# First norm and projections of a two-layer trunk: both token halves together, in six banks

## The chip, the cores and the metric

The kernel runs on one core of a Trainium2 chip. The metric is the time of one execution on the device, in microseconds (us). Five engines work side by side, each through its own list of instructions in a fixed order: PE (TensorE, matrix products and transposes), DVE (VectorE), ACT (ScalarE), POOL (GpSimd) and SP (SyncE, which here issues the DMAs). They wait for each other by semaphores. SBUF holds the operands, PSUM the sums of PE, in eight banks; in this kernel a bank holds 128 rows of 512 fp32 numbers.

## The reference

The input x has 1024 tokens (S) of 1024 features (D). There are two layers; the first mixes tokens by attention with a forget gate (16 heads of 64), the second by gated linear attention, and each ends with a feed-forward layer. Every sub-layer begins with an RMS norm, whose result is scaled and shifted by columns that come from a conditioning vector c. All is fp32. Only the start of the first layer matters here:

```python
c_act = jax.nn.silu(c)
mod = c_act @ ada_w[i] + ada_b[i]                  # 1024 x 6144 weights
sh1, sc1, g1, sh2, sc2, g2 = jnp.split(mod, 6, axis=-1)
h = modulate(rms_norm(x, norm1_g[i]), sh1, sc1)    # norm * (1 + sc1) + sh1
proj = h @ w_in
q, k, v, f_logit = jnp.split(proj, [D, 2 * D, 3 * D], axis=-1)
log_f = jax.nn.log_sigmoid(f_logit + b_f)
cum = jnp.cumsum(log_f, axis=1)                    # over the tokens
logits = q @ k^T * scale + cum[query] - cum[key]   # per head, causal, softmax, times v
```

So the first scores need all of x normed, sh1 and sc1 of every feature, the f logits of all tokens (the running sum `cum`), and q and k of the first heads.

## The kernel before

Features are cut into eight tiles of 128 (index d), tokens into eight tiles of 128 (`xt[0]` to `xt[7]`), which form two halves of 512 (`hf` 0 and 1). Products of fp32 numbers are made of three matmuls: every operand is split into a high part and a low part, and `mm3` (L236–239) adds high × high, high × low and low × high into one bank.

The part before attention works as follows.

- `load_x` (L274) loads a token tile, 512 KB; `load_ada0` (L280) loads the columns of `ada_w` for sh1 and sc1 of one feature tile d in four DMAs of 256 KB. All go out on SP's queue, in the order in which they stand there.
- `ss_half(hf)` (L436) makes the norm of one half: ACT squares and sums four token tiles (L439), DVE and POOL make the reciprocal root (L441, L442), and the four tiles are scaled in place. In the first half DVE, ACT and POOL share that work; in the second POOL scales all four (L450).
- `ada0_mod(d)` (L455) makes sh1 and sc1 of feature tile d. That is a product of a 1024 × 256 piece of `ada_w` with the vector c. For the first `NPE[d]` of its eight row blocks PE does it directly (L462); the rest is summed on DVE by one instruction for each block (L468, L470), and PE adds the rows of the sum (L472). DVE then writes `modc` (L473) and `amul` (L333), the shift and the scale columns.
- `h_block(d, hf)` (L476) transposes four blocks of 128 × 128 of one half on PE (L479) into a bank of the ring `tp0`, ACT applies scale and shift (L481: `y`) and rounds it to the high part `h0h` (L483), and DVE (even d) or POOL (odd d) subtracts to get the low part `h0l` (L484).
- `first_k(d, hf, acc)` (L489) adds feature tile d into the f, q and k banks of one half: two matmuls for f (L491, L492) and three each for q and k (L237 to L239), 128 × 512 each. q and k are those of the first two heads.
- `first_v` (L811) adds feature tile d into the v banks of the first half, 12 matmuls of 128 × 256 (L817 to L819).
- `first_evac` (L776) empties the f, q and k banks. For the second half it also makes `log_f`, its running sum (a scan along the tokens), writes that to DRAM and loads it back, spread over the partitions (`load_cum`, L802).
- `v_half(g, half)` (L855) computes v of a half for group g of heads, by token tiles; its banks come from the ring `pj` of the attention stage, which are the last two of the eight.
- `load_w` (L190) loads a weight tile and splits it: ACT rounds, POOL subtracts three quarters and DVE one quarter (L205). `feed.next()` calls it for the next weight tiles in line.

In this order: first the norm of the first half, then the loop over d (L829 to L852), in which each pass makes the columns and `h_block` of d + 1, `first_k(d, 0)` and `first_v(d − 1)`; at d = 4 (`XD`) the second half's token tiles are loaded and normed. Behind the loop the first half is evacuated, and a second loop runs `h_block` and `first_k` of the second half. Then come v of the second half (`v_half(0, 1)`), and attention, in which the q and k of the next heads are woven between the scores. `ada0.q` holds the steps for the other columns of the first layer's modulation (`ada_steps`, L336; on DVE L367, L369), which fill in from there.

The program is written in this order, and a scheduler then fixes the order of each engine's list, moving an instruction ahead of others where it reckons that engine free. So the lists hold, for instance, matmuls of v between those of the second half.

PSUM before attention: the ring `par` has five banks (f, q, k and the two v accumulators of the first half, then f, q, k of the second half), `tp0` two banks for transposes, `mp0` one for the columns.

Of the kernel before, what the change touches and what calls it, by code (L numbers as in the profile page):

```python
# [9 lines left out]
F32 = mybir.dt.float32  # L10
# [6 lines left out]
P = 128  # L17
# [36 lines left out]
def trunk(ctx, tc, x, c, ada_w, ada_b, norm1_g, norm2_g, ffn_w_in, ffn_w_out,  # L54
          fox_w_in, fox_b_f, fox_w_out, gla_w_in, gla_w_a2, gla_b_a, gla_g_o,
          gla_w_out, final_g, out, dbg=None, stop=None):
    nc = tc.nc
# [209 lines left out]
    adr = Ring(big, adr_sl + mrows[1:] + acc_sl + s1_sl)  # L267
    mrows = Views(mrows[:1], 8, [P], "mrows").v
    wst = Ring(big, take(6))
    par, tp0, mp0 = ps_rings(5, 2, 1)  # L270

    xt = [xr([P, D], F32, f"xt{t}") for t in range(8)]

    def load_x(t):  # L274
        nc.sync.dma_start(xt[t], x[0, psl(t), :])
# [4 lines left out]
    def load_ada0(d):  # L280
        for kh in range(2):
            t = adr([P, 4, 2, P], F32, f"adas{d}{kh}")
            for j in range(2):
                nc.sync.dma_start(t[:, :, j, :], adaw[0, :, 4 * kh:4 * kh + 4, j, d, :])
            araw[(d, kh)] = t
# [20 lines left out]
    wq0 = load_w(W[:, 0:P], "wq0", wst)  # L306
    wk0 = load_w(W[:, D:D + P], "wk0", wst)
    load_ada0(1)
    load_ada0(2)

    vps = mp0([P, 160], F32, "vps")
    nc.tensor.transpose(vps[:, P:P + 32], rows2, ident[0:32, 0:32])
# [23 lines left out]
    def ada_steps(l, j, acc_of, raw_of, w):  # L336

        steps = deque((c0, k) for c0 in range(0, D, w) for k in range(8))
        got = deque()

        def load():
            if steps:
                c0, k = steps.popleft()
                raw = raw_of([P, w], F32, f"ada{l}{j}{c0}{k}")
                nc.sync.dma_start(raw, ada_w[l, psl(k), j * D + c0:j * D + c0 + w])
                got.append(raw)

        for c0 in range(0, D, w):
            acc = acc_of([P, w], F32, f"acc{l}{j}{c0}")
            for k in range(8):  # L350
                if w == D or c0 == k == 0:
                    load()
                raw = got.popleft()
                if w < D:
                    load()
                    yield ADA_A
                    if k == 0:
                        nc.scalar.mul(acc, raw, cact[:, 0:1])
                    else:
                        nc.scalar.mul(raw, raw, cact[:, k:k + 1])  # L360
                        nc.gpsimd.tensor_add(acc, acc, raw)  # L361
                    yield ADA_B
                    continue
                for q in range(0, w, 256):
                    cs = slice(q, q + 256)
                    if k == 0:
                        nc.vector.tensor_scalar(acc[:, cs], raw[:, cs], cact[:, 0:1], None, op0=ALU.mult)  # L367
                    else:
                        nc.vector.scalar_tensor_tensor(acc[:, cs], raw[:, cs], cact[:, k:k + 1], acc[:, cs],  # L369
                                                       op0=ALU.mult, op1=ALU.add)  # L370
                yield 1.0
            if w < D:
                yield ADA_B
            n, b = w // P, c0 // P
            mp = pj([P, n], F32, f"mp{l}{j}{c0}")
            for k in range(n):
                nc.tensor.matmul(mp[:, k:k + 1], acc[:, psl(k)], ones, start=True, stop=True)
            o = l * 48 + j * 8 + b
            nc.vector.tensor_add(modc[:, l, j, b:b + n], mp, vec[:, o:o + n])
# [54 lines left out]
    hT = new_h("h0")  # L434
# [14 lines left out]
            else:  # L449
                nc.gpsimd.tensor_scalar(xt[t], xt[t], r, 1.0, op0=ALU.mult, op1=ALU.mult)  # L450

    VLAG, XD = 1, 4
    NPE = (4, 4, 4, 0, 0, 0, 0, 0)

    def ada0_mod(d):  # L455

# [19 lines left out]
    def h_block(d, hf):  # L476
        tp = tp0([P, HALF], F32, f"xp{d}{hf}")
        for i in range(4):
            nc.tensor.transpose(tp[:, psl(i)], xt[4 * hf + i][:, psl(d)], ident)  # L479
        y = yv()  # L480
        nc.scalar.activation(y, tp, AF.Identity, scale=acol(0, 0, d), bias=mcol(0, 0, d))  # L481
        hi, lo = hT[d].hi[:, hsl(hf)], hT[d].lo[:, hsl(hf)]
        nc.scalar.copy(hi, y)  # L483
        (nc.gpsimd if d % 2 == 1 else nc.vector).tensor_sub(lo, y, hi.bitcast(F32))  # L484

    def first_acc(hf):
        return [(w, par([P, HALF], F32, f"{nm}s{hf}")) for nm, w in (("f", wf), ("q", wq0), ("k", wk0))]

    def first_k(d, hf, acc):  # L489
        ps = acc[0][1]  # L490
        nc.tensor.matmul(ps, wf[:, d, :], hT[d].hi[:, hsl(hf)], start=d == 0, stop=False)  # L491
        nc.tensor.matmul(ps, wf[:, d, :], hT[d].lo[:, hsl(hf)], start=False, stop=d == 7)  # L492
        for w, ps in acc[1:]:
            mm3(ps, w.hi[:, d, :], w.lo[:, d, :], hT[d].hi[:, hsl(hf)], hT[d].lo[:, hsl(hf)], d == 0, d == 7)
# [271 lines left out]
    feed = Weights(loads)  # L766
# [6 lines left out]
    vts = {}  # L773
    wvs = {}

    def first_evac(hf, acc):  # L776
        cs = hsl(hf)
        f = zt[:, cs]
        sum16(f, ze[:, cs], acc[0][1])
        nc.scalar.activation(ze[:, cs], f, AF.Abs, bias=bf)  # L780
        nc.vector.tensor_scalar(zt[:, cs], f, bf, 0.0, op0=ALU.add, op1=ALU.min)
        nc.scalar.activation(ze[:, cs], ze[:, cs], AF.Exp, scale=-1.0)
        if hf:
            nc.scalar.activation(ze, ze, AF.Ln, bias=1.0)
            nc.vector.tensor_sub(zt, zt, ze)
            nc.vector.tensor_tensor_scan(cum, zt, zt, 0.0, ALU.add, ALU.bypass)
            nc.sync.dma_start(cum_d, cum)
            load_cum(0)
            load_cum(1)
        q_evac(acc[1][1], qkt[0], hf)  # L790
        k_evac(acc[2][1], qkt[0], hf)

    def v_split(g, tp, ps):
        v = vring([P, 2, 4, 2, 64], FR, f"v{g}{tp}")
        src = ps.rearrange("p t (h d) -> p t h d", h=4)
        for i in range(2):
            split(v[:, i, :, 0, :], v[:, i, :, 1, :], src[:, i])
        vts[g].append(v)
# [4 lines left out]
        cums[h] = cumr([P, S], F32, f"cum{h}")  # L803
        nc.sync.dma_start(cums[h], cum_d[h].partition_broadcast(P))

    vts[0] = []
    ss_half(0)
    acc = first_acc(0)
    vacc = [par([P, 2, 256], F32, f"vps0{tp}") for tp in range(2)]

    def first_v(d):  # L811
        wv = wvs[0][d // 4]
        for tp in range(2):
            for i in range(2):
                ts_ = psl(2 * tp + i)
                p_, a_ = vacc[tp][:, i, :], (hT[d].hi[:, ts_], hT[d].lo[:, ts_])
                nc.tensor.matmul(p_, a_[0], wv.hi[:, d % 4, :], start=d == 0 and i == 0, stop=False)  # L817
                nc.tensor.matmul(p_, a_[0], wv.lo[:, d % 4, :], start=False, stop=False)
                nc.tensor.matmul(p_, a_[1], wv.hi[:, d % 4, :], start=False, stop=d == 7 and i == 1)  # L819

    def pre(d):
        ada0_mod(d)
        if d + 3 < 8:
            load_ada0(d + 3)
        h_block(d, 0)

    pre(0)
    for d in range(8):
        if d == 0:  # L829
            feed.depth = 1  # L830
            wvs[0] = [feed.next()]
        if d == 2:
            wvs[0].append(feed.next())
        if d < 7:
            pre(d + 1)
        first_k(d, 0, acc)
        if d >= VLAG:
            first_v(d - VLAG)
        if d == XD:
            for t in range(4, 8):  # L840
                load_x(t)
            ss_half(1)
    for d in range(8 - VLAG, 8):
        first_v(d)
    first_evac(0, acc)
    acc = first_acc(1)
    for tp in range(2):
        v_split(0, tp, vacc[tp])
    h_block(0, 1)
    for d in range(8):  # L850
        if d < 7:
            h_block(d + 1, 1)  # L852
        first_k(d, 1, acc)
    first_evac(1, acc)
    def v_half(g, half):  # L855

        if g not in vts:
            vts[g] = []
        if g not in wvs:
            wvs[g] = [feed.next(), feed.next()]  # L860
        for tp in range(2 * half, 2 * half + 2):
            ps = pj([P, 2, 256], F32, f"vps{g}{tp}")
            for i in range(2):
                yield from proj_tok(ps[:, i, :], wvs[g], hT, 2 * tp + i)
            v_split(g, tp, ps)
        if g or half:
            del wvs[g]
# [122 lines left out]

    for j in (2, 3, 4, 5):
        ada0.q.append(ada_steps(0, j, acc_r, wr, D))
    run(v_half(0, 1))
    for p in range(7):
        parts = [qk_proj(p + 1, 0), qk_proj(p + 1, 1)]
# [757 lines left out]
    wv = [feed.next(), feed.next()]  # L1753
# [18 lines left out]
    for h in range(4):  # L1772
# [102 lines left out]
```

## Time and profile before

| What | us |
|---|---|
| median of three runs | 2450.28 (2445.8 to 2456.89) |
| profiled execution | 2455.79 |
| its span | 2454.1 |
| PE busy | 2393.3 |
| DVE busy | 1697.8 |
| ACT busy | 1193.6 |
| POOL busy | 1153.2 |

The span is the time from the first to the last record of the profile; the profiled execution's own time is a little longer than the span. Busy times are sums over the instructions of an engine. In the rows, a name such as `L472` is a line of the code before, `out<-in` names the tiles, `x4` is a number of records (an fp32 matmul leaves two), and what stands in brackets is the idle time ahead of an instruction and what ended it. The profile's `issue` stands for time in which an engine waited for nothing that the records show. The granted clock is TensorE's, as a share of full speed, averaged over the stretch.

### The profile page before, as it was taken

What the parts mean: (1) busy time and instruction counts of PE and PEld (TensorE: products, weight loads), DVE (VectorE), ACT (ScalarE), POOL (GpSimd) and SP (SyncE); (2) the same over time, 40 slices, a digit from 0 to 9 for tenths busy, and PEclk for the clock granted to TensorE, in tenths of its full rate; (3) what the DMA queues carried; (4) which work ended last, traced back from release to release, by engine and by line L of the source; (5) the groups of instructions that cost most, each with busy time, mean ns of one, the idle gap of its engine ahead of it and who ended that gap; (6) DMA issues with size and microseconds to landing.
All of it is one profiled execution on the core that took longest, in us unless ns stands there. A gap on an engine that the chain in (4) does not pass through costs nothing.

```text
span 2454.1 us, 35528 instructions
## 1 busy us (share of the span) xinstructions
PE 2393.3 (98%) x12458; PEld 2038.0 (83%) x12458; DVE 1697.8 (69%) x2849; ACT 1193.6 (49%) x2281; POOL 1153.2 (47%) x1006
## 2 busy tenths in 40 slices
PE   6999999999999999999999999999999999999998
PEld 6788888888887878888888888888888888888888
DVE  6477777776687777665787555446587767665787
ACT  4565665675454443345324765564344333435325
POOL 4233333332348776653263634442326666653362
PEclk9999999999999999999999999999999999999999
DMA  8223333233426554347665333335325444347664
GB/s 268 79 87 121 96 98 117 70 95 112 131 99 204 180 170 162 129 173 256 233 202 169 100 95 95 95 104 172 102 72 195 143 137 153 125 160 265 229 213 148
DMA packets 318203, 359.19 MB, mean 146 GB/s; under 512 B 18044, under 2 KB 246552, under 8 KB 318024
## 3 DMA queue, kind: packets, MB, share of 16 engines
q1 hardware_dynamic: 318024, 356.92, 43.7%
q8 instruction: 98, 1.61, 0.3%
q14 instruction: 81, 0.66, 0.1%
HBM read 268.19 MB, written 88.67 MB: 145 GB/s over the span
## 4 chain that ended last, share of the span: by engine, by line
PE 79%; DVE 8%; DMA 4%; ACT 3%; POOL 3%; issue 2%; SPq 0%; DVEq 0%; POOLq 0%; ACTq 0%
PE p_b L237 14%; PE p_b L239 14%; PE p_b L238 14%; PE o_b L947 2%; PE t_b L933 2%; PE qk_b L237 2%; PE qk_b L238 2%; PE qk_b L239 2%; DMA ad_s<-in_ada_w_dram 2%; POOL ad_s L361 1%; PE s_b L902 1%; PE s_b L903 1%; PE vps_b L237 1%; PE vps_b L239 1%; PE vps_b L238 1%
## 5 line engine op out<-in xcount | busy, mean ns | idle before, releaser
L160 DVE TENSOR_TENSOR o_s<-xv_s,o_s 128x512 fp32r<-128x512 f32 (+1 forms) x376 | 326.4, 872 | 87.5 <-ACT o_s L159 87.0
L159 ACT CAST o_s<-xv_s 128x512 fp32r<-128x512 f32 (+1 forms) x376 | 217.4, 587 | 304.4 <-PE p_b L239 261.2
L237 PE MATMUL p_b<-B,o_s 128*128 128x512 f32 x608 | 237.2, 393 | 6.3 <-DVE x L1285 3.8
L238 PE MATMUL p_b<-B,o_s 128*128 128x512 f32 x608 | 238.3, 392 | 0.0
L239 PE MATMUL p_b<-B,o_s 128*128 128x512 f32 x608 | 238.0, 392 | 0.0
L913 POOL TENSOR_SCALAR lp_s<-lp_s,st 128x128 f32<-128x128 f32 (+7 forms) x128 | 96.0, 756 | 295.2 <-DVE st L912 274.9
L683 POOL TENSOR_TENSOR ex_s<-xv_s,xv_s 128x512 f32<-128x512 f32 (+1 forms) x64 | 90.6, 1415 | 255.1 <-DMA xv_s<-in_ffn_w_in_dram 93.2
L237 PE MATMUL p_b<-T,o_s 128*128 128x512 f32 x480 | 187.4, 391 | 0.0
L238 PE MATMUL p_b<-T,o_s 128*128 128x512 f32 x480 | 186.8, 389 | 0.0
L239 PE MATMUL p_b<-T,o_s 128*128 128x512 f32 x480 | 182.0, 389 | 0.0
L237 PEld LDWEIGHTS p_b<-B,o_s 128*128 128x128 f32 x608 | 115.2, 189 | 31.4 <-DVE x L1285 3.2
L239 PEld LDWEIGHTS p_b<-B,o_s 128*128 128x128 f32 x608 | 115.0, 189 | 24.1
L238 PEld LDWEIGHTS p_b<-B,o_s 128*128 128x128 f32 x608 | 115.2, 189 | 23.7
L911 ACT ACTIVATE lp_s<-lp_s,st 128x128 f32<-128x128 f32 (+7 forms) x128 | 99.3, 776 | 56.8 <-DVE st L907 56.4
L1285 DVE TENSOR_TENSOR ex_s<-ex_s,p_b 128x512 f32<-128x512 f32 x140 | 94.0, 681 | 36.5 <-PE p_b L239 36.3
L159 ACT CAST pt_s<-t_b 128x512 fp32r<-128x512 f32 (+1 forms) x160 | 80.1, 547 | 71.0 <-PE t_b L933 69.8
L685 POOL TENSOR_TENSOR xv_s<-ex_s,xv_s 128x512 f32<-128x512 f32 (+1 forms) x64 | 84.4, 1318 | 61.0 <-DVE o_s L160 58.8
L160 DVE TENSOR_TENSOR pt_s<-t_b,pt_s 128x512 fp32r<-128x512 f32 (+1 forms) x160 | 96.6, 631 | 17.7 <-ACT pt_s L159 17.0
L239 PEld LDWEIGHTS p_b<-T,o_s 128*128 128x128 f32 x480 | 90.1, 188 | 18.9
L237 PEld LDWEIGHTS p_b<-T,o_s 128*128 128x128 f32 x480 | 90.1, 188 | 18.5
L238 PEld LDWEIGHTS p_b<-T,o_s 128*128 128x128 f32 x480 | 90.2, 188 | 18.4
L907 DVE CUSTOM_DVE_ANT_0 lp_s<-s_b,cum_s 128x512 f32<-128x512 f32 (+3 forms) x128 | 72.7, 570 | 41.7 <-PE t_b L933 22.9
(1939 smaller groups left out, 7561.4 us busy)
## 6 DMA issues: line engine op xcount, KB each, us to landing
xv_s<-in_ffn_w_in_dram SPq DMA_DIRECT2D x176, 256.0 KB, 3.0
hid_B<-x SPq DMA_DIRECT2D x70, 512.0 KB, 2.6
ad_s<-in_ada_w_dram SPq DMA_DIRECT2D x96, 256.0 KB, 2.9
hid_T<-x SPq DMA_DIRECT2D x36, 512.0 KB, 2.7
xv_s<-in_ffn_w_out_dram SPq DMA_DIRECT2D x96, 192.0 KB, 4.1
ada_s<-in_ada_w_dram SPq DMA_DIRECT2D x32, 512.0 KB, 3.9
xv_s<-in_ffn_w_out_dram SPq DMA_DIRECT2D x40, 256.0 KB, 2.9
T2o<-hid_T SPq DMA_DIRECT2D x18, 512.0 KB, 8.1
```

The costliest lines, as they stand in the source:

```text
L159: nc.scalar.copy(hi, src)
L160: nc.vector.tensor_sub(lo, src, hi.bitcast(F32))
L237: nc.tensor.matmul(ps, ah, bh, start=start, stop=False)
L238: nc.tensor.matmul(ps, ah, bl, start=False, stop=False)
L239: nc.tensor.matmul(ps, al, bh, start=False, stop=stop)
L683: nc.gpsimd.tensor_add(s1, a21, a22)
L685: nc.gpsimd.tensor_sub(a11, s1, a11)
L907: nc.vector.tensor_tensor_reduce(lp[:, k0:k1], ps, cm[:, k0:k1], 1.0, mcur, ALU.add, ALU.min, mnew)
L911: nc.scalar.activation(lp, lp, AF.Exp, bias=mcur, scale=-1.0, accum_out=st[:, qi, 2:3])
L913: nc.gpsimd.tensor_scalar(lp, lp, st[:, qi, 3:4], 1.0, op0=ALU.mult, op1=ALU.mult)
L933: nc.tensor.transpose(tp[:, i, :], lps[qi][:, psl(2 * b + jj)], ident)
L1285: nc.vector.tensor_add(d, d if src is None else dest(G, src), ps)
```

## The change

- PSUM: `par` gets six banks, f, q and k for both halves at once; `tp0` keeps one bank for transposes instead of two.
- Token tiles 4 to 7 are loaded at the start, behind the ada columns of tile 1 and ahead of those of tile 2. The ada columns of tile 3 are asked for at the start too, and in the loop the columns are loaded four tiles ahead instead of three.
- `NPE[2]` is 0 instead of 4: the column sums of tile 2 are made on DVE altogether.
- One loop of ten passes takes both halves: pass d makes the columns and `h_block` of d + 1 for the first half, `first_k(d, 0)`, then `first_k(d − 2, 1)` and `h_block(d − 1, 1)` for the second. The second half's norm stands in pass 0, the two weight tiles of v are asked for in passes 3 and 5, and the first half is evacuated in pass 7.
- `first_v` is gone: `v_half(0, 0)` computes v of the first half behind the loop, and `v_half(0, 1)` that of the second behind it, as before. The number of matmuls of v is the same.

```diff
-    par, tp0, mp0 = ps_rings(5, 2, 1)
+    par, tp0, mp0 = ps_rings(6, 1, 1)
...
     load_ada0(1)
+    for t in range(4, 8):
+        load_x(t)
     load_ada0(2)
+    load_ada0(3)
...
-    VLAG, XD = 1, 4
-    NPE = (4, 4, 4, 0, 0, 0, 0, 0)
+    NPE = (4, 4, 0, 0, 0, 0, 0, 0)
...
-    vts[0] = []
     ss_half(0)
-    acc = first_acc(0)
-    vacc = [par([P, 2, 256], F32, f"vps0{tp}") for tp in range(2)]
-
-    def first_v(d):
...
+    accs = [first_acc(hf) for hf in range(2)]
 
     def pre(d):
         ada0_mod(d)
-        if d + 3 < 8:
-            load_ada0(d + 3)
+        if d + 4 < 8:
+            load_ada0(d + 4)
         h_block(d, 0)
 
+
+    feed.depth = 1
     pre(0)
-    for d in range(8):
-        if d == 0:
-            feed.depth = 1
-            wvs[0] = [feed.next()]
-        if d == 2:
-            wvs[0].append(feed.next())
+    for d in range(10):
         if d < 7:
             pre(d + 1)
-        first_k(d, 0, acc)
-        if d >= VLAG:
-            first_v(d - VLAG)
-        if d == XD:
-            for t in range(4, 8):
-                load_x(t)
+        if d < 8:
+            first_k(d, 0, accs[0])
+        if d == 0:
             ss_half(1)
-    for d in range(8 - VLAG, 8):
-        first_v(d)
-    first_evac(0, acc)
-    acc = first_acc(1)
-    for tp in range(2):
-        v_split(0, tp, vacc[tp])
-    h_block(0, 1)
-    for d in range(8):
-        if d < 7:
-            h_block(d + 1, 1)
-        first_k(d, 1, acc)
-    first_evac(1, acc)
+        if d in (3, 5):
+            wvs.setdefault(0, []).append(feed.next())
+        if d == 7:
+            first_evac(0, accs[0])
+        if d >= 2:
+            first_k(d - 2, 1, accs[1])
+        if 1 <= d < 9:
+            h_block(d - 1, 1)
+    first_evac(1, accs[1])
+
...
+    run(v_half(0, 0))
     run(v_half(0, 1))
```

More of the change, by code (lines that the diff above doesn't have):

```diff
@@ L804, in load_cum @@
         nc.sync.dma_start(cums[h], cum_d[h].partition_broadcast(P))
-    vts[0] = []
     ss_half(0)
-    acc = first_acc(0)
-    vacc = [par([P, 2, 256], F32, f"vps0{tp}") for tp in range(2)]
-    def first_v(d):
-        wv = wvs[0][d // 4]
-        for tp in range(2):
[L814 to L819, printed above, removed]
+    accs = [first_acc(hf) for hf in range(2)]
     def pre(d):
         ada0_mod(d)
-        if d + 3 < 8:
-            load_ada0(d + 3)
+        if d + 4 < 8:
+            load_ada0(d + 4)
         h_block(d, 0)
+    feed.depth = 1
     pre(0)
-    for d in range(8):
-        if d == 0:
-            feed.depth = 1
-            wvs[0] = [feed.next()]
-        if d == 2:
-            wvs[0].append(feed.next())
+    for d in range(10):
         if d < 7:
             pre(d + 1)
-        first_k(d, 0, acc)
-        if d >= VLAG:
-            first_v(d - VLAG)
-        if d == XD:
-            for t in range(4, 8):
-                load_x(t)
-            ss_half(1)
-    for d in range(8 - VLAG, 8):
-        first_v(d)
-    first_evac(0, acc)
-    acc = first_acc(1)
-    for tp in range(2):
-        v_split(0, tp, vacc[tp])
-    h_block(0, 1)
-    for d in range(8):
-        if d < 7:
-            h_block(d + 1, 1)
-        first_k(d, 1, acc)
-    first_evac(1, acc)
+        if d < 8:
+            first_k(d, 0, accs[0])
+        if d == 0:
+            ss_half(1)
+        if d in (3, 5):
[7 more added lines that the diff above has]
+    first_evac(1, accs[1])
     def v_half(g, half):
```

## The prediction

> **What bounds the kernel now.** I read the page's totals first, then the busy time in stretches of the start, then what PE waited for there, then the chain of waits. Only the first 130 us of the kernel are touched by the change, so the question is how far along PE is when it leaves them.
>
> The page's span and totals; then the view by stretches (start:end, length, busy us and instructions of PE, PEld, DVE, ACT, POOL, the granted clock, the DMA share and rate):
>
> ```profile
> span 2454.1 us, 35528 instructions
> PE 2393.3 (98%) x12458; PEld 2038.0 (83%) x12458; DVE 1697.8 (69%) x2849; ACT 1193.6 (49%) x2281; POOL 1153.2 (47%) x1006
> ```
> ```profile
> 0.00:25.00 25.00, 11.97 (x52) 11.05 (x53) 10.97 (x26) 12.25 (x19) 9.70 (x17) 1.00 0.91 265
> 25.00:60.00 35.00, 30.39 (x169) 27.09 (x167) 29.11 (x63) 15.66 (x26) 15.65 (x17) 1.00 0.87 280
> 60.00:75.00 15.00, 10.28 (x44) 8.71 (x45) 10.52 (x21) 5.92 (x10) 6.12 (x7) 0.66 0.37 115
> 75.00:110.00 35.00, 34.19 (x220) 30.65 (x219) 15.26 (x23) 24.13 (x41) 6.80 (x5) 1.00 0.09 28
> 110.00:130.00 20.00, 18.34 (x101) 14.46 (x101) 12.77 (x36) 10.72 (x22) 10.09 (x13) 1.00 0.44 135
> 130.00:150.00 20.00, 20.00 (x157) 18.97 (x155) 14.38 (x43) 12.54 (x29) 9.30 (x15) 1.00 0.21 58
> 150.00:200.00 50.00, 50.00 (x332) 44.41 (x331) 36.20 (x97) 28.54 (x61) 14.88 (x20) 1.00 0.37 115
> 20.00:30.00 10.00, 9.60 (x37) 8.77 (x38) 6.77 (x17) 2.38 (x4) 3.40 (x6) 1.00 1.10 331
> ```
>
> PE is busy 98% of the span, and from 130 to 200 us without a gap. Work that PE has not done by 130 us is therefore done later at full price: a delay at the start carries to the end one for one. What there is to win or lose is PE's idle time: 4.6 us (35.00 − 30.39) in 25–60, 4.7 in 60–75, 0.8 in 75–110 and 1.7 in 110–130. In 25–60 DVE is nearly as busy (29.1 of 35) as PE, and the DMA runs at 280 to 331 GB/s: the modulation (ada) columns arrive at that rate and DVE reduces them.
>
> What PE waited for from 24 to 75 us (total, times, longest), and the chain of waits:
>
> ```profile
> PE mp_b L472 <- DVE acc L470: 5.3, 1, 5.3
> PE xp_b L479 <- POOL xt_s L450: 2.3, 2, 1.3
> ```
> ```profile
> 58.33 1.25 DVE acc L470
> 59.58 3.12 DVE acc_s L367 x3
> 62.70 0.60 DVE h0l L484
> 63.85 0.98 PE mp_b L472 x4
> 68.63 0.43 PE qs_b L238
> 70.98 0.23 PE qs_b L237
> 72.35 0.12 PE vps_b L819
> 97.95 0.58 ACT ze_s L219
> 112.44 5.60 DMA cum_s<-cum_d
> 118.51 0.34 DVE lp_s L907
> ```
>
> The one long wait (5.3 us) is for the last ada tile: its DVE chain at 63.3 gates the modulation column of feature tile 7. After it, matmuls cost 0.43 us until about 70.6 instead of 0.23: the stretch with granted clock 0.66. The f logits of the second half end at 97.95; from there to the running sum of log f used on DVE at 118.5 lies a chain of 20.5 us, which PE fills with v and the next q, k.
>
> **The change part by part.** More rows, from the timeline (start, us, engine, line, operation):
>
> ```profile
> 28.96 3.58 PE L462 MATMUL mp_b<-cact,adas_s 128*128 128x1 f32 x16 [0.25 <-DVE modc L473]
> 37.77 0.60 PE L479 MATMUL xp_b<-ident,xt_s 128*128 128x128 f32 x4
> 118.65 0.47 PE L902 MATMUL s_b<-KA,QA 128*128 128x512 f32 x1 [0.49 <-DVE st L907]
> ```
> ```profile
> 29.10 0.15 DVE L333 SCALAR_TENSOR_TENSOR amul<-modc,vec 128x1 f32<-128x1 f32 x1
> 29.22 2.05 DVE L470 SCALAR_TENSOR_TENSOR acc<-adas_s,cact,acc 128x256 f32<-128x256 f32 x4
> 35.22 0.15 DVE L333 SCALAR_TENSOR_TENSOR amul<-modc,vec 128x1 f32<-128x1 f32 x1
> ```
> ```profile
> 29.35 0.78 ACT L481 ACTIVATE y_s<-xp_b,modc,amul 128x512 f32<-128x512 f32 x1 [7.59 <-DVE amul L333]
> 49.60 1.06 ACT L439 ACTIVATE sq_s<-xt_s 128x1024 bf16<-128x1024 f32 x1
> 55.58 4.99 POOL L450 TENSOR_SCALAR xt_s<-xt_s,rstd 128x1024 f32<-128x1024 f32 x4
> 61.25 1.31 POOL L484 TENSOR_TENSOR h0l<-y_s,h0h 128x512 fp32r<-128x512 f32 x1
> 40.41 2.25 SPq L275 DMA_DIRECT2D xt_s<-in_x_dram  x4
> 65.79 0.45 SPq L345 DMA_DIRECT2D ada_s<-in_ada_w_dram  x1
> ```
>
> *Loads.* The four x tiles (2 MB, at 331 GB/s about 6.3 us) move on SP's queue from behind the ada tiles to behind ada(1), and push ada(2) and later ones, and the weights of v, back by that much. The total is unchanged, so ada(7) still lands at about 53. ada(1) landed at about 22, so x4–x7 are there by 28.5, and ada(2) at about 31.5 instead of 25.5. That alone is no loss: DVE reaches ada(2) later anyway (below). Loading ada(3) up front only fixes the order.
>
> *Squares and scaling of the second half.* Four squares on ACT (1.06 each plus a read) end at about 29.3, when amul(1) is ready: y(1) slips by 0 to 0.7 us. Then POOL scales four tiles for 5 us, at about 30.7–35.7 instead of 55.6–60.6. While POOL did so, DVE finished one instruction per 1.13 to 1.25 us (rows at 58.33 above, and 3 in 3.12) instead of 4 in 2.05. That slow-down moves from 55–61 to 31–36.
>
> *ada(2) on DVE.* NPE[2] goes from 4 to 0: eight fp32 matmuls on PE (16 records, 3.58 us at the cold price) go, four more DVE steps of 0.5 us come. In the changed order DVE first computes the second half's rstd (waits for the squares, about 30), and then the last step of ada(2) is the tenth instruction, since steps of ada(3) stand between. One alone 0.5, four under the scaling (5.0), one under POOL's h0l(1) (1.3), four at 0.5 would give 30.1 + 8.8 = 38.9; 38.1 if more fit beside h0l. I take 38.1; amul(2) follows three instructions later, about 41 instead of 35.2. PE, which has only tile 0 and 1's matmuls to do, stands at mp(2) from about 31.6: +6.5 us.
>
> *The following tiles.* DVE now has eight steps for each d (4 us) plus h0l (0.68), and the splits of three weight tiles share POOL and DVE: amul(3) 47, amul(4) 53.5, amul(5) 58.7. Between them PE has 16 matmuls (two halves, 8 × 0.23 each) plus two sets of transposes (0.44 each): about 4.6 us, less than the 5 to 6.5 us of a DVE step. That leaves PE waits of about 3.1 us at mp(5) (49.3–52.4), 6.2 us for h0l(4), which DVE computes behind two interleaved ada chains and the split (58.4–64.5), and 1.1 at the transposes of tile 2, which with a single bank now wait for y of the block before (0.78). All in all 17 to 17.5 us idle in 25–75 against 9.3 before (4.6 + 4.7). That is the size I trust least: its nearest rows bound the extra between −9.3 (no waits) and about +15 (each of five DVE rounds of 6.5 us against 4.6 of PE work, +9.5, and the 6.5 at mp(2), with nothing taken back).
>
> *Cold clock.* The first cold stretch lasts longer (to about 43 instead of 36.5) with the same work in it; the second (60.4–70.6 now) shrinks to about 63.8–67.2, which saves 2 to 1 us; I take 1.
>
> *Bank and v.* Values leave the loop: the same 192 matmuls of 0.12 us, later, where they fill the wait for the running sum in place of the next q, k. No cost as such; but what stood there comes later.
>
> Sum by idle time: +7.9 − 3.6 − 1 = +3.3. Sum by position: at 64.5 PE still has, up to the first score that needs the running sum, 77 matmuls at 0.23 (17.7), 28 transposes at 0.11 (3.1), 192 of v at 0.12 (23.0), 16 of the next q, k (3.7), some 4.5 of small ones and 1.6 for the cold rest: 64.5 + 53.6 = 118.1, against 118.65. But by then the kernel before had done 44 of the next q, k matmuls, the changed one 16: 28 × 0.23 = 6.4 behind; up to 1.7 us idle in 110–130 is filled in return. That gives 118.1 − 118.65 + 6.4 − 1.7 = +4.2 (+5.9 without the filling). I take +4.5: the profiled execution took 2455.8, so 2460.3 by it; it lies 5.5 above the median of the runs, 2450.28, so 2455 for the median.
>
> A rule to weigh. The Trainium skill, "TensorE: Matmul & The Clock Gate", section "Why this matters for your kernels", says that gaps of PE of more than about 3 us between bursts bring the half clock back. The rows at 63.85–70.98 agree (a 5.3 us wait, then 0.43 for 2 us of matmuls and more). By it each of the new waits of 6 us would be followed by a slow stretch; that is rival A.
>
> **The rivals.**
>
> A. The stop and go keeps the clock at half. Before, one 5.3 us wait was followed by matmuls of 0.43. The changed kernel would have such waits at 31.6, 49.3 and 58.4. About 15 us of PE work lies between 43 and 67 at 0.23; at 0.43 it takes 13 us more, of which the waits behind absorb half: +6 on top of the forecast, about 2461. For it: the row pair 68.63 / 70.98. Against: in 25–60 the granted clock reads 1.00 with short waits in it.
>
> B. Slower by over 0.5%: DVE's queue holds modc(7). Sixteen steps of the next modulation (L367, 0.5 us each, 7.7 us in all) now stand ahead of modc(7), and the last four need a fourth tile whose DMA leaves only once the first tile is used (65.79 before) and lands 4 to 6 us later. By my count modc(7) is ready at 75.4, just when PE reaches the first v matmul in the bank that mp(7) holds; every us past it costs PE a us, and the f chain behind. It decides from 8 us late: +12.5, 2463 and up. Against: in the row at 59.58 those steps pass quickly when POOL is quiet.
>
> C. Faster: DVE keeps up, since both halves give PE 16 matmuls for each tile. Then the idle 9.3 us, 2.2 us of cold matmuls and the 3.6 of L462 go, less some 3 at mp(2): −12, about 2438. For it: the 5.3 us wait of before came from DVE's slow stretch under POOL's scaling, which is no longer there. Against: DVE busy 29.1 of 35 us already, with four fewer steps.
>
> D. Not PE's position but the running sum decides at 118: f's second half ends up to 3.5 us sooner, so attention starts sooner: −3.5, about 2447. Against: from 130 to 200 PE has no idle time to give back.
>
> **How the numbers follow.** Half a percent, 12.3 us, is about what a measurement of this kernel can tell from no change. The forecast (2455, its own range 2450 to 2460) gets 0.46, A 0.16, B 0.18, C 0.08, D 0.12. Faster than 2438: most of C and the edge of D, 0.09. Slower than 2462.5: B, half of A and an edge of the forecast's waits, 0.32. The rest, 0.59, within. The range 2441 to 2469 leaves out half of C and the far end of B.
>
> **What would show it.** In the changed profile: POOL's scaling at 30–36 us with DVE steps of 1.2 us beside it; amul(2) at about 41 (35.2 means the first term is wrong); PE waits of 6.5 us at mp(2) and about 6 us before h0l(4); PE idle of 17 us in 25–75; no long cold stretch at 60–70; f of the second half done at 95–98.6; the first score at 117–119, with the next q, k 28 matmuls behind. From 200 us on the two profiles run alike, shifted. I am wrong if DVE keeps 0.5 us steps beside POOL (C), if the clock stays at half between the waits (A), or if PE waits for modc(7) (B).

## The result

The changed kernel takes 2459.28 us in the median of 8 runs (2452.14 to 2462.95), the kernel before 2449.74 (8 runs beside it). The ratio is 1.0031, with a 95% interval of 1.0018 to 1.0044: 0.31% slower, 7.6 us with an interval of 4.4 to 10.8 (the two medians themselves lie 9.5 us apart). In a second series it was 1.0031 again (1.0016 to 1.0047). The prediction had +4.5 us, and a chance of 0.59 for a change of under half a percent either way.

The lines of the code behind the norm have moved by two or three: L333 is L336 now, L450 is L453, L470 is L472, L472 is L474, L484 is L486; the store of a finished head pair, L974, is L956. The page of the changed kernel, its stretches, and what PE waited for from 24 to 75 us:

```profile
span 2452.5 us, 35504 instructions
PE 2387.6 (97%) x12442; PEld 2031.5 (83%) x12442; DVE 1704.2 (69%) x2853; ACT 1195.3 (49%) x2281; POOL 1150.4 (47%) x1006
```
```profile
25.00:60.00 35.00, 21.62 (x95) 16.36 (x94) 32.14 (x59) 16.40 (x26) 19.83 (x20) 0.80 0.83 252
60.00:75.00 15.00, 13.64 (x64) 11.75 (x65) 11.89 (x30) 4.20 (x6) 2.62 (x3) 0.77 0.62 187
75.00:110.00 35.00, 32.94 (x232) 30.29 (x231) 14.65 (x22) 21.49 (x35) 3.87 (x3) 1.00 0.01 3
110.00:130.00 20.00, 19.27 (x107) 15.68 (x105) 9.84 (x30) 12.48 (x26) 9.65 (x13) 1.00 0.34 106
130.00:150.00 20.00, 19.37 (x158) 18.86 (x159) 14.03 (x42) 10.52 (x27) 6.67 (x13) 1.00 0.26 79
```
```profile
PE mp_b L474 <- DVE acc L472: 6.6, 1, 6.6
PE fs_b L494 <- DVE h0l L486: 5.4, 1, 5.4
PE mp_b L474 <- DVE modc L475: 0.9, 1, 0.9
```

PE's idle time in 25 to 75 us is 14.7 us (13.38 + 1.36), 9.3 before. Two waits make most of it, and both are for DVE. The timeline shows where they stand and what DVE and POOL did there:

```profile
28.16 4.78 DVE L472 SCALAR_TENSOR_TENSOR acc<-adas_s,cact,acc 128x256 f32<-128x256 f32 x5
38.34 0.15 DVE L336 SCALAR_TENSOR_TENSOR amul<-modc,vec 128x1 f32<-128x1 f32 x1
71.70 0.16 DVE L336 SCALAR_TENSOR_TENSOR amul<-modc,vec 128x1 f32<-128x1 f32 x1
28.86 5.07 POOL L453 TENSOR_SCALAR xt_s<-xt_s,rstd 128x1024 f32<-128x1024 f32 x4
36.41 0.98 PE L474 MATMUL mp_b<-ones,acc 128*128 128x1 f32 x4 [6.61 <-DVE acc L472]
61.36 0.80 PE L494 MATMUL fs_b<-h0l,fw_s 128*128 128x512 f32 x1 [5.39 <-DVE h0l L486]
115.72 0.39 PE L884 MATMUL s_b<-KA,QA 128*128 128x512 f32 x1
```

The last amul (tile 7) is ready at 71.70; before it was at 65.39. Yet the whole time of one execution says little here: the profiled execution of the changed kernel has a span of 2452.5, less than the 2454.1 of the one before, though the medians stand the other way. So I measure the early part by a landmark in it, the second store of a finished head pair (SP's queue), which both kernels issue behind the same work. First before, then after:

```profile
253.09 0.33 SPq L974 DMA_DIRECT2D oT_d<-oT_s  x1
```
```profile
256.90 0.33 SPq L956 DMA_DIRECT2D oT_d<-oT_s  x1
```

That is +3.8 us. Most of it is there at the first such store (187.93 before, 191.28 after, +3.4), and it is kept: at the same transfer of the feed-forward stage (hid_B, 1032.34 before, 1035.95 after) it is +3.6.

### The profile page after: what moved, and what is told of

It is laid out like the page before. It is cut to its first block, busy times and chain, and to the rows that moved or that the text cites. A ratio compares the mean times of both kernels' runs of the same rounds, so it can differ in the third digit from the quotient of the medians.

```text
span 2452.5 us, 35504 instructions
## 1 busy us (share of the span) xinstructions
PE 2387.6 (97%) x12442; PEld 2031.5 (83%) x12442; DVE 1704.2 (69%) x2853; ACT 1195.3 (49%) x2281; POOL 1150.4 (47%) x1006
## 4 chain that ended last, share of the span: by engine, by line
PE 57%; POOL 3%; DVE 3%; ACT 2%; DMA 2%; issue 2%; POOLq 0%; SPq 0%; DVEq 0%; ACTq 0%
PE p_b L237 14%; PE p_b L239 14%; PE p_b L238 14%; DMA ad_s<-in_ada_w_dram 2%; POOL ad_s L364 1%; PE gr_b L237 1%; PE gr_b L239 1%; PE gr_b L238 1%; PE gv_b L239 1%; PE gv_b L237 1%; PE gv_b L238 1%; PE gk_b L237 1%; PE gk_b L238 1%; PE gk_b L239 1%; ACT ad_s L363 0%
## 5 line engine op out<-in xcount | busy, mean ns | idle before, releaser
L893 ACT ACTIVATE lp_s<-lp_s,st 128x128 f32<-128x128 f32 (+7 forms) x128 | 99.3, 776 | 63.8 <-DVE st L889 61.1
L205 POOL TENSOR_TENSOR w_l_s<-w__s,w_h_s 128x256 fp32r<-128x256 f32 x90 | 69.7, 803 | 67.4 <-ACT w_h_s L202 57.9
```

What stands on the lines that cost most here:

```text
L205: (nc.gpsimd if i < 3 else nc.vector).tensor_sub(lo[:, cs], rw[:, cs], hi[:, cs].bitcast(F32))
L893: nc.scalar.activation(lp, lp, AF.Exp, bias=mcur, scale=-1.0, accum_out=st[:, qi, 2:3])
```

## Experiments

Theory 1 was: the loss is made by PE's waits before 75 us, which DVE's queue causes, and is carried on one for one. The rivals of it stand with each run. The store's time is that of the landmark above; the kernels of e1 to e4, of e5 to e8, and of e9 to e12 ran together, each set on one chip.

### e1: the changed kernel again

> The changed kernel once more, unaltered, with its own profile. Theory 1 (the loss is made in the first 75 us by PE's waits and carried on): the second oT store (256.90 in its profile, 253.09 before) stands again at 256 to 258, and the ratio to the kernel before is 1.001 to 1.004. Rival (the +9.5 us between the medians is made elsewhere too): landmarks between 600 and 2400 us drift away from before's by more than the 4 us that stand at 600.

Ratio 1.0031 (1.0016 to 1.0047). The profile of this execution (stretches, waits at the same two places, store, and the later landmark):

```profile
25.00:60.00 35.00, 23.66 (x100) 18.38 (x99) 30.09 (x57) 17.55 (x28) 18.97 (x20) 1.00 0.82 254
60.00:75.00 15.00, 11.88 (x58) 10.12 (x59) 13.35 (x31) 3.58 (x5) 3.35 (x4) 0.77 0.67 201
38.36 0.98 PE L474 MATMUL mp_b<-ones,acc 128*128 128x1 f32 x4 [5.38 <-DVE acc L472]
63.12 0.80 PE L494 MATMUL fs_b<-h0l,fw_s 128*128 128x512 f32 x1 [5.43 <-DVE h0l L486]
257.73 0.33 SPq L956 DMA_DIRECT2D oT_d<-oT_s  x1
1043.31 0.34 SPq L1201 DMA_DIRECT2D hid_B<-x  x1
```

The two waits, the idle time (14.5 us) and the store come out as before: +4.6. But at 1043.31 this execution is 11.0 us behind, not 3.6. From store to landmark it took 785.6 us, against 779.1 in the first execution of the changed kernel and 779.3 in that of the kernel before. So there is a second source of difference, 6.5 us in this execution, which varies from one to the next. Both statements of the expectation hold, the rival's for this execution. Where those 6.5 us went is shown below, under the clock.

### e2: tile 2 partly back on PE

```diff
-    NPE = (4, 4, 0, 0, 0, 0, 0, 0)
+    NPE = (4, 4, 4, 0, 0, 0, 0, 0)
```

> Changed kernel with four row blocks of tile 2's columns back on PE. Theory 1 (DVE's chain under POOL's scaling holds PE at mp(2)): PE does the eight matmuls inside the wait, the fifth instead of the tenth DVE instruction ends the chain, the wait of 6.6 us falls to under 1 us, mp(2) stands at 33 to 34 instead of 36.4, and the second oT store comes 2 to 3 us earlier (254 to 255). Rival (PE's waits before 75 us are hidden by the 20 us of the running sum's chain): the store stays at 256 to 258.

```profile
30.42 1.20 DVE L470 TENSOR_SCALAR acc<-adas_s,cact 128x256 f32<-128x256 f32 x1 [1.28 <-DMA adas_s<-in_ada_w_dram]
36.70 1.01 PE L474 MATMUL mp_b<-ones,acc 128*128 128x1 f32 x4 [4.34 <-DVE acc L472]
256.42 0.33 SPq L956 DMA_DIRECT2D oT_d<-oT_s  x1
```

The expectation missed, and the store lies in the range of its rival. The wait fell from 5.4 (e1) to 4.3 only, the store came 0.5 to 1.3 us earlier, not 2 to 3 (and that is within the landmark's scatter, see e5), and the ratio is 1.0026 (1.0013 to 1.0040). With four steps fewer DVE began with the second half of the columns, and for that it had to wait: the DMA had not brought it (1.28 us idle, and then steps of 1.2 beside POOL's scaling). The token tiles had gone ahead of it on the same queue, which the prediction had called no loss because DVE would come late anyway. The run does not refute the rival by itself: PE idles 2.7 us less in 25–75 than in e1 (11.8), but 1.95 us of that are the matmuls that came back.

### e3: ACT scales the second half

```diff
-            elif hf == 0 and t == 1:
+            elif hf == 1 or t == 1:
                 nc.scalar.activation(xt[t], xt[t], AF.Copy, scale=r)
```

> Changed kernel with the four scalings of the second half on ACT instead of POOL. Theory 1: DVE keeps 0.5 us for a step, the tenth instruction ends at about 33, the wait at mp(2) falls from 6.6 to about 3 us and the second oT store comes 3 us earlier (about 254). Rival (the steps are slow because the DMA brings the columns late, not because of POOL): steps stay at 1.2 us or wait for the DMA, and mp(2) stays at 36.

```profile
30.75 3.47 DVE L472 SCALAR_TENSOR_TENSOR acc<-adas_s,cact,acc 128x256 f32<-128x256 f32 x5
35.82 0.98 PE L474 MATMUL mp_b<-ones,acc 128*128 128x1 f32 x4 [0.37 <-DVE acc L472]
60.65 1.01 PE L474 MATMUL mp_b<-ones,acc 128*128 128x1 f32 x4 [4.56 <-DVE acc L472]
255.97 0.33 SPq L956 DMA_DIRECT2D oT_d<-oT_s  x1
```

The five steps take 3.47 us instead of 4.78: POOL's scaling was the brake, as far as it went. The wait at mp(2) is almost gone (0.37), and the wait for DVE at about 60 is still there, now at mp(6) (4.56). The store comes 0.9 to 1.8 us earlier than in the changed kernel, where 3 were expected; the ratio is 1.0016 (1.0004 to 1.0029).

### e4: the subtraction that PE waited for, on POOL

```diff
-        (nc.gpsimd if d % 2 == 1 else nc.vector).tensor_sub(lo, y, hi.bitcast(F32))
+        (nc.gpsimd if d % 2 == 1 or (d, hf) == (4, 0) else nc.vector).tensor_sub(lo, y, hi.bitcast(F32))
```

> Changed kernel with the low part of tile 4, first half, on POOL instead of DVE. Theory 1 (PE stood 5.4 us because that subtraction was queued on DVE behind two ada chains and weight splits): that wait falls to 1 to 3 us, and a new one of 2 to 4 us comes at mp(6), whose chain on DVE is unchanged; gain 1 to 2.5 us at the second oT store. Rival (the wait is for ACT's y or the transposes): the wait stays over 4 us.

```profile
65.28 1.01 PE L474 MATMUL mp_b<-ones,acc 128*128 128x1 f32 x4 [5.48 <-DVE acc L472]
259.71 0.33 SPq L956 DMA_DIRECT2D oT_d<-oT_s  x1
```

The wait for h0l(4) went, and one of the same length, 5.5 us, stood at mp(6). The store came 2.0 to 2.8 us later, not earlier, and the ratio is 1.0045 (1.0027 to 1.0063). So the place at which PE stands is incidental: it is DVE's chain of columns that is late. Theory 1 holds in that form; the gain that I expected of this edit was wrong in sign. The added POOL operation did not make that chain later: amul(6) came at 68.90, in e1 at 69.62, with amul(1) at 29.42 and 29.50. Against e1, whose store is 2.0 us earlier, PE idles 0.9 us more in 25–75 (15.4), and from 53.7 to 57.0 the granted clock is 0.50, where e1 has 1.00.

### e5: the kernel before again

> The kernel before once more, with its own profile. If the drift that the changed kernel showed between 700 and 900 us in one of its two profiles (+4.6 at 573 us, +10.97 at 1032 us) is a matter of the single execution, two executions of the kernel before differ there by several us as well. The second oT store (253.09) moves with the start by 1 to 2 us at most.

One run took 2450.01 us. The store stands at 252.72, 0.4 us from that of the first profile, and PE waits 5.3 us at the last tile again. The changed kernel's two profiles lie 3.8 to 5.0 us behind the two of before. Pairs of executions of one kernel lie 0.4 us apart here, 0.8 in e1 and 2.0 in e6 and e12, so differences of the store under 2 us between single profiles tell little. The two executions of the kernel before do not show a jump of the size of e1's between the landmarks (778.3 and 779.3 us).

### e6 and e12: the kernel before with ACT scaling

The edit of e3 on the kernel before, in two series.

> Kernel before with the second half's four scalings on ACT instead of POOL. Theory 1 (DVE's queue, slowed while POOL scales, makes PE's 5.3 us wait at the last tile): the wait falls to 1 to 3 us, the two waits for POOL's scaling (2.3 us) go, the slow stretch 60-71 gets shorter, and the second oT store comes 3 to 5 us earlier than 253.09, a gain of 0.1 to 0.2%. Rival (the wait is for the last ada tile's DMA, landed at about 53): the wait stays over 4 us, no gain.

> The kernel of e6 once more (kernel before with the second half scaled on ACT), to see whether the 5.4 us that it gains in the first 130 us reach the end. Theory 1 (what is gained by 130 us is kept one for one): the second oT store at 247 to 249, both series together 0.9975 to 0.999. Rival (a later stage gives it back): store at 247 to 249, but both series together at 0.9995 to 1.000.

What PE waited for longest in 24 to 75 us in e6, and the stores of e6 and e12:

```profile
PE fs_b L492 <- POOL h0l L484: 1.8, 1, 1.8
```
```profile
247.71 0.33 SPq L974 DMA_DIRECT2D oT_d<-oT_s  x1
```
```profile
249.70 0.33 SPq L974 DMA_DIRECT2D oT_d<-oT_s  x1
```

The 5.3 us wait is gone, and so are the two for POOL: the longest is 1.8. The store comes 3.0 to 5.4 us earlier; that of e12 stands later than the 247 to 249 which both its theories expected. In the time of the whole kernel that is not resolved: 0.9994 (0.9984 to 1.0005) and 0.9992 (0.9981 to 1.0003). Both lie between what the two theories expected of the series together. This is the best version seen, but that it beats the kernel before is shown up to the store only.

### e7: the early norm alone, in the kernel before

```diff
     load_ada0(1)
+    for t in range(4, 8):
+        load_x(t)
     load_ada0(2)
...
-        if d == XD:
-            for t in range(4, 8):
-                load_x(t)
+        if d == 0:
             ss_half(1)
```

> Kernel before with one part of the change alone: token tiles 4 to 7 loaded behind ada(1) and the second half's norm made in pass 0; two transpose banks, v in the loop and NPE as before. Theory 1: amul(2) goes from 35.2 to 38 to 40 because POOL's scaling stands beside DVE there; PE has v's matmuls to do but still waits about 3 us; the wait of 5.3 us at the last tile shrinks as DVE is undisturbed at 55-60. Sum: second oT store between -2 and +2 us of 253.09. Rival (the early norm is what costs the +4): the store comes 4 us later.

```profile
251.56 0.33 SPq L974 DMA_DIRECT2D oT_d<-oT_s  x1
```

amul(2) went to 39.11 and the store to 251.56, 1.2 to 1.5 us before that of the kernel before; the ratio is 1.0000 (0.9989 to 1.0011). The early loads and the early norm, which cost the changed kernel its wait at mp(2), cost nothing in the loop of the kernel before: there PE waits 3.4 and 1.4 us for DVE at mp(2) and mp(3), and in exchange the 5.3 us wait at the last tile goes; over 25–75 PE idles 9.6 us, as in the kernel before (9.3 and 9.6). (This execution began early, with amul(1) at 27.41 instead of 29.10, so that the 1.2 to 1.5 us are no gain to rely on.) They are not the cause of the loss by themselves.

### e8 and e9: half of the column sums on PE

Both are e3 with `NPE = (4, 4, 4, 4, 4, 4, 4, 4)`, which takes 24 steps off DVE.

> Changed kernel with ACT scaling the second half and four row blocks of every tile's columns on PE: 24 DVE steps of 0.5 us fewer, 6 times 1.95 us more for PE. Theory 1 in its sharper form (DVE's queue bounds 30 to 65 us, PE's place of waiting is incidental): PE's idle time in 25-75 (14.5 us in the repeat) falls to 2 to 5 us, the added 11.7 us of PE work take its place, no slow stretch after 45, second oT store 254 to 256. Rival (PE's waits come from the order of work, transposes and the single bank): idle stays over 8 us and the store comes later than 258.

PE's row at its longest wait in e8, and DVE's row ahead of it:

```profile
58.70 3.58 PE L464 MATMUL mp_b<-cact,adas_s 128*128 128x1 f32 x16 [4.10 <-DVE modc L475]
54.90 3.68 DVE L370 TENSOR_SCALAR acc_s<-ada_s,cact 128x256 f32<-128x256 f32 x4 [1.91 <-DMA ada_s<-in_ada_w_dram]
266.41 0.33 SPq L956 DMA_DIRECT2D oT_d<-oT_s  x1
```

Theory 1 missed: PE's idle time in 25–75 is 7.6 us, between the two expectations, and the store was 9 us later than the changed kernel's, with a ratio of 1.0050 (1.0036 to 1.0064). DVE had time, but its list has four steps of the next modulation ahead of the column of tile 4, and those waited for their DMA. That is the mechanism of the prediction's rival B, in a kernel where DVE is early enough to run into it. e9 keeps these steps back:

```diff
+    nc.vector.scalar_tensor_tensor(cactL, modc[:, 0, 0, 0:8], 0.0, cact, op0=ALU.mult, op1=ALU.add)
     for j in (2, 3, 4, 5):
         ada0.q.append(ada_steps(0, j, acc_r, wr, D))
...
-                        nc.vector.tensor_scalar(acc[:, cs], raw[:, cs], cact[:, 0:1], None, op0=ALU.mult)
+                        nc.vector.tensor_scalar(acc[:, cs], raw[:, cs], cactL[:, 0:1], None, op0=ALU.mult)
```

> As e8 (ACT scales the second half, four row blocks of every tile on PE), but the steps of the next modulation (L370, L372) take c from a copy that is written only after the last column, so that none of them can stand ahead of a column on DVE. If e8 was slow because DVE waited there for the DMA of those steps with the column of tile 4 behind them: no modc waits for a DMA, amul(7) comes at 64 to 68 (75.8 in e8), PE's idle time in 25-75 falls under 6 us, and the second oT store stands at 256 to 259 instead of 266.41. Rival (the 11.7 us of extra PE work are what e8 lost): the store stays at 264 to 267.

```profile
25.00:60.00 35.00, 29.67 (x132) 25.92 (x132) 16.43 (x34) 17.59 (x26) 12.96 (x15) 0.69 1.05 284
262.74 0.33 SPq L957 DMA_DIRECT2D oT_d<-oT_s  x1
```

No column stood behind a step of the next modulation any more, and PE's idle time in 25–75 fell to 5.3 us, as expected. DVE still waited for the DMA of the columns themselves, 6.9 us in four waits from 25 to 80, and amul(7) came at 76.73, not at 64 to 68 (the 75.8 given for e8 is its tile 6; its amul(7) came at 80.69). The store stands at 262.74, between the two expectations, and the ratio is 1.0073 (1.0051 to 1.0094). DVE is busy for 16.4 of 35 us here and no longer the bound; PE is, with the one-column matmuls and at a clock of 0.69. So DVE's column sums did make PE's waits in the changed kernel, and handing half of them to PE costs more than the waits did.

### e10: the same hold in the changed kernel

> Changed kernel, with only the steps of the next modulation held back behind the last column. Rival B of the prediction (these steps hold modc(7) and PE with it): amul(7) comes 3 us or more earlier than 72.7 and the second oT store 2 to 4 us earlier than 257.73. Theory 1 (PE gets to mp(7) no sooner, the columns of tiles 2 to 6 set its pace): amul(7) 0 to 2 us earlier, the store within 1 us.

amul(7) came at 69.50 instead of 72.71 (e1; 71.70 in the first profile), and the store at 256.69, 0.2 us before that of the first profile and 1.0 before that of e1; the ratio is 1.0037 (1.0023 to 1.0052). amul(7) moved as rival B said, the store as theory 1 said: PE did not wait for it.

### e11: v of the first half out of the loop, alone

```diff
-        if d >= VLAG:
-            first_v(d - VLAG)
...
+    run(v_half(0, 0))
     run(v_half(0, 1))
```

> Kernel before with v of the first half taken out of the loop and computed behind both halves, as in the change, all else as before (five banks and two, second half in a second loop). If v is what filled PE's time while DVE makes the columns: PE's idle time in 25-75 (9.3 to 9.6 us before) grows by 4 to 8 us and the second oT store (253.09, 252.72) comes 3 to 7 us later. Rival (v falls into other waits, so its place is free): idle within 2 us, the store within 1.5 us.

```profile
25.00:60.00 35.00, 26.56 (x117) 20.49 (x116) 29.28 (x64) 15.34 (x26) 15.92 (x17) 0.85 0.77 254
255.99 0.33 SPq L955 DMA_DIRECT2D oT_d<-oT_s  x1
```

PE's idle time in 25–60 is 8.4 us (4.6 in the first profile of before, 5.6 in e5), and the store comes 2.9 to 3.3 us later, the lower edge of what the filler theory expected; over 25–75 the idle time grew by 2.0 to 2.2 us only, less than expected. The ratio is 1.0014 (1.0001 to 1.0027). Of the two parts that were tried alone in the kernel before (e7 and this one), this is the one that costs.

### The clock in later stages

e1 lost 6.5 us between 258 and 1043 us that the other execution of the same kernel did not. The rows of the stretches, e1 first and then the first profile of the changed kernel:

```profile
753.50:760.20 6.70, 5.58 (x13) 4.42 (x14) 2.51 (x5) 3.03 (x7) 2.65 (x2) 0.50 0.63 194
876.40:879.60 3.20, 2.76 (x7) 2.18 (x8) 1.51 (x3) 2.14 (x4) 2.07 (x2) 0.50 0.82 290
688.60:691.80 3.20, 3.20 (x11) 2.62 (x10) 0.00 (x0) 0.00 (x0) 0.00 (x0) 0.50 0.00 0
```
```profile
753.50:760.20 6.70, 6.70 (x33) 5.59 (x32) 5.28 (x7) 2.94 (x5) 4.62 (x3) 1.00 0.51 152
876.40:879.60 3.20, 3.20 (x19) 2.75 (x18) 2.84 (x5) 0.85 (x2) 0.88 (x1) 1.00 0.42 139
688.60:691.80 3.20, 3.20 (x20) 2.77 (x19) 0.99 (x2) 0.21 (x1) 0.10 (x1) 1.00 0.00 0
```

In e1 the clock was at half for 6.7, 3.2 and 3.2 us there; in the other execution the granted clock is 1.00 in all three stretches. The waits before them are of the same kind: e1's at 876 was shorter than that of the other execution at 871, which brought no slow stretch:

```profile
876.84 0.79 PE L237 MATMUL p_b<-B,o_s 128*128 128x512 f32 x1 [2.56 <-DVE sg_s L1268]
```
```profile
870.82 0.50 PE L237 MATMUL p_b<-B,o_s 128*128 128x512 f32 x1 [2.75 <-DVE sg_s L1268]
```

PE was busy for 5.58 + 2.76 + 3.20 = 11.5 us in these stretches; half of that, 5.8 us, is most of the 6.5 us. The Trainium skill, "TensorE: Matmul & The Clock Gate", Part 1, says that activity is judged in free-running windows of about 3.4 us; the stretches, near one and two of those, agree, and so does a 2.56 us pause that counts where one of 2.75 does not. In each trace the changes of the granted clock lie whole multiples of 3.41 us apart. Cut at these places, the two executions differ in where the pause falls, e1 first:

```profile
872.90:876.30 3.40, 1.38 (x7) 0.80 (x5) 3.40 (x5) 0.63 (x1) 2.74 (x2) 1.00 0.46 157
```
```profile
866.00:869.40 3.40, 2.07 (x10) 1.37 (x8) 3.40 (x5) 0.63 (x1) 2.75 (x2) 1.00 0.42 166
869.40:872.80 3.40, 1.98 (x9) 1.65 (x10) 1.70 (x3) 2.00 (x4) 1.62 (x3) 1.00 0.93 300
```

In e1 PE was busy for 1.38 of 3.40 us, and half clock follows; in the other the longer pause lies across two such stretches, which have 2.07 and 1.98 us of work, and the clock stays full. So the rule that the prediction weighs, by the length of a gap, does not hold here as it stands: 2.56 us were enough, and 2.75 were not.

## Why the prediction was right, point by point

**Sign, size, range.** The forecast was slower by 4.5 us and not clear of noise, range 2441 to 2469. Measured were 2459.28, +7.6 with an interval of 4.4 to 10.8. The forecast lies at the lower edge of the interval. That its size is near the early loss is in part luck, as the terms below show. At the landmark, which the prediction argued about, it is 3.8 and 4.6 us against the profile of before (3.8 to 5.0 with e5).

**What bounds.** That the first 130 us count one for one holds between 250 and 570 us (the last store of a head pair, 568.13 before, comes 4.4 and 4.5 us later); for the whole time the profiles confirm it only within the scatter of the later stages. e6 and e12 gained 3.0 to 5.4 us early and their times do not resolve it.

**Squares and POOL's scaling.** Forecast 30.7–35.7, measured 28.86–33.93, with all of this execution's early work some 2 us ahead (amul(1) at 27.1, 29.1 before); the five steps beside it took 4.78 us, 3.47 in e3 without POOL's scaling. Right. amul(2) came at 38.34, and at 40.30 in e1; the forecast was about 41.

**The wait at mp(2).** Forecast 6.5; 6.6 and 5.4 (e1). Its cause, DVE's chain beside POOL's scaling, holds: e3 takes the wait down to 0.37. In the changed kernel no step of ada(2) waits for its DMA by as much as 0.2 us. The step "That alone is no loss" holds only as long as DVE does all eight blocks: with four of them on PE, DVE waits 1.28 us for the DMA (e2).

**The following tiles.** Forecast 6.2 us for h0l(4): 5.4 and 5.4. At mp(5) 3.1 was forecast: 0.9 and 2.2 (e1). All idle time in 25–75: forecast 17 to 17.5, measured 14.7 and 14.5. So the term +7.9 was mis-sized: it is +5.2 or +5.4. (The bound of the extra, "about +15", adds up to 16.)

**Bank and v.** The prediction gave the removal of v "No cost as such". e11 shows a cost, +2.9 to +3.3 us at the store: in the loop of before, the matmuls of v fill part of PE's waits, and without them PE stands idle there (8.4 us in 25–60, 4.6 and 5.6 before). The forecast has these waits under the following tiles, so it had the effect, but not the part of the change that makes it.

**Behind 75.** Not forecast: 2.1 us idle in 75–110 (0.8 before) and 0.6 in 130–150 (none before). In 110–130 0.7 are idle against 1.7 before, where the forecast had up to all of it filled. Together +0.9 us. The sum by idle time with these sizes is +5.2 + 0.9 − 3.6 − 1 = +1.5, too little. The last two terms are the ones that fail. The 3.6 was the price of the eight matmuls at the slow clock; in e5 they took 1.95 us, and slow clock came behind them instead (32.5 to 35.8). At the slow price matmuls stand 0.43 us apart instead of 0.23, so half of PE's busy time in the slow stretches is an estimate of what the clock cost: from 25 to 150 us 8.6 and 6.7 us in the two profiles of before, 7.1 and 8.0 in the two of the changed kernel. That is no saving beyond the scatter. What is left is the idle time, 18.2 and 18.1 us from 25 to 150 against 11.8 and 12.4, and the 1.95 us of matmuls: +6.1 − 1.95 = +4.1, against 3.8 to 5.0 at the store. The forecast's +3.3 came near it because waits that were too long stood against savings that did not come.

**Position.** The first 128 x 512 score came at 115.72 (116.72 in e1), before the forecast 117 to 119; 16 matmuls of the next q, k were done by then, as forecast, and 44 in the kernel before. Behind its score the kernel before idles 1.17 us up to 130, and the changed one 0.73 and then 0.63 in 130–150 (0.71 and 0.84 in e1). The same sum then gives 115.72 − 118.65 + 6.4 + 0.2 = +3.7, and +4.9 for e1, against +3.8 and +4.6 at the store. The prediction took off all of the 1.7 us in 110–130, of which 0.5 lies ahead of 118.65 and was in the position already. This sum was the right one to make: it counts work done, whatever the clock was.

**Cold clock.** Rival A's long slow stretch did not add to the forecast: slow matmuls stood after both long waits (36.4 to 43.4, and 61.4 to 67.2), the first as the forecast had it, the second from 61.4 instead of 63.8; none stood at mp(5), where PE waited 0.9 and 2.2 us. The row that the prediction sets against A, a granted clock of 1.00 in 25–60, says less than it seems (last section).

**Rival B** did not decide: modc(7) was ready when PE came, and e10 shows no more than 1 us in it, within the scatter. Its mechanism is real (e8). **Rival C** did not come: DVE is busy 32.1 of 35 us. **Rival D**: the sum of log f left for DRAM earlier (108.33, 110.21 before), and attention still ended later; what decides there is PE's position.

**What stays open.** The time is 7.6 us longer, the early part 3.8 to 5.0. The difference lies within the interval of 4.4 to 10.8. e1 shows where such a rest can come from, but not that the changed kernel meets more slow stretches on average. Estimated as above, the slow clock behind 250 us cost 13.6 and 6.8 us in the two profiles of before, and 10.2 and 16.0 in those of the changed kernel; without it the spans are 2440.5 and 2441.5, and 2442.2 and 2444.4. Of the parts, v's place is the one that showed a loss alone (e11, +2.9 to +3.3 at the store); the early norm showed none (e7), tile 2's columns 0.5 to 1.3 (e2), within the scatter. What remains was not assigned. The sixth accumulator bank and the single bank for transposes were not tried alone.

## What to carry to other kernels

When an engine waits behind another engine's queue, moving the one operation it stands at only moves the wait (e4); look for the chain that is late. Before taking filler out of a loop that is paced by another engine, price what the engine that loses the filler will do in its waits (e11). And measure a change in the first tenth of a kernel by a landmark behind it: two executions agreed to between 0.4 and 2.0 us there, while whole times scattered by ten.

## What the runs showed of the hardware

A stretch in which PE was hardly idle was followed by half clock, if its matmuls had one moving column. In e1, thirty records of such matmuls stand in the second row, in which PE is busy throughout, and the next row is at half speed:

```profile
682.15 3.77 PE L512 MATMUL sp_b<-ones,ss_s 128*128 128x1 f32 x30
681.70:685.10 3.40, 3.40 (x30) 3.18 (x28) 0.35 (x1) 1.32 (x2) 1.48 (x1) 1.00 0.45 182
685.30:688.40 3.10, 3.10 (x9) 2.61 (x10) 0.16 (x1) 0.00 (x0) 1.02 (x1) 0.50 0.00 0
```

The same is seen in e5 (PE busy 3.08 us from 29.1 to 32.4, of which 1.95 are the eight matmuls of a tile's columns, then half clock from 32.5) and in e9 (3.15 us from 28.4 to 31.8, then 13.5 us at half). So matmuls with one moving column hardly count as activity, and four row blocks on PE are dearer than their 1.95 us, in line with e9's loss.

The Trainium skill, "TensorE: Matmul & The Clock Gate", Part 4 ("PE-mode transpose"), says that the full clock does not engage for transposes, which do not count as busy in the same way. Here they do count. In this row of e5, PE did nothing but transposes and four records of one-column matmuls (0.51 us), and the granted clock is 1.00 in the next 3.3 us too, in which PE is idle:

```profile
2438.80:2442.20 3.40, 2.34 (x20) 1.87 (x17) 1.41 (x4) 1.37 (x4) 0.54 (x1) 1.00 0.00 0
```

Cut at the places where the clock can change, the fourteen traces have 9761 stretches of 3.41 us at full clock, of which 116 are followed by half clock. With one-column matmuls left out, PE was busy for at most 0.54 of each of the 116, and for at least 0.44 of each of the others.

One more thing for reading: the column of the granted clock reads 1.00 for 25–60 in the kernel before and in e1, though single matmuls there took the slow price at first (0.43 us apart up to about 36 and 43). The record of the clock begins with its first change, at 36.5 us in the profile of before and at 43.5 in e1, and a stretch ahead of that reads 1.00 whatever the clock was. The durations of the rows are the surer sign.
